# First layer's modulation vectors: more of their rows on VectorE, fewer and larger visits on TensorE

## The chip, the cores and the metric

The kernel runs on one core of a Trainium2 chip. The metric is device time in microseconds (us) of one execution, the median of several. TensorE (PE in the profile) does the matmuls; VectorE (DVE) and ScalarE (ACT) work on tiles in SBUF and on the matmuls' results in PSUM; SyncE (SP, its queue is SPq) issues the transfers from HBM, in the order in which they stand in its program. GpSimd does nothing here.

## The reference

Two layers of a diffusion backbone, float32 in and out, 256 latent tokens and 256 context tokens of 2048 channels. Each layer modulates its normalised input by vectors that it first computes from a conditioning vector (one for the latent stream, one for the context):

```
shift, scale, gate = split(silu(c) @ ada_w[l] + ada_b[l], 3)
h  = rmsnorm(x,  norm_g[l]) * (1 + scale)   + shift
hc = rmsnorm(xc, norm_g[l]) * (1 + scale_c) + shift_c
... = split(h @ w_in[l])        # then attention, pooling, Fourier mixing, gate, w_out
```

`ada_w[l]` is 2048 x 6144. For layer 0, nothing of the input projection can start before shift and scale are there, so the kernel computes these 4096 columns (33.5 MB of weights) piece by piece while it already multiplies the channels whose modulation is known. Two vectors (latent and context) are multiplied by each weight, so this product is bound by reading the weights, not by arithmetic.

## The kernel before, in words

**Pieces.** Activations lie with channels on the 128 partitions: 16 tiles of 128 channels by 512 tokens (`KT = 16`). In `startup` (lines 743 to 926) the 16 tiles are taken in ten groups, `GROUPS = (1, 1, 2, 2, 2, 2, 2, 2, 1, 1)`, numbered 0 to 9 below. A group of two tiles needs 512 columns of `ada_w` (256 shift, 256 scale), over 2048 contraction rows. The rows are cut in quarters; a quarter is one transfer of 1 MB (512 KB in a group of one tile) into the tile `a0`. This document writes **piece 5.1** for quarter 1 of group 5. The tile `a0` has four buffers (`ST = 4`), shared by all pieces: a transfer into a buffer waits until the last reader of that buffer's earlier contents is done.

**On TensorE**, a piece is one visit (line 891): four float32 matmuls, side by side in four 32-column strips of the array, with the conditioning vectors `cs` as the stationary operand. Between visits `work(n)` puts out `n` matmuls of the backlog (line 828): the first layer's input projection, three float32r products per term, over the channel tiles that are ready. After the last visit of a group ScalarE copies the sums from PSUM (`ev`, line 894), and four matmuls with a 0/1 matrix `selt` (line 897) turn the row vectors to columns and add the four strips. VectorE adds the bias and the norm's gain (lines 902 to 910), giving `ab`.

**Modulation.** `make_h` (line 244) multiplies a tile by the inverse root mean square (line 249), scales and shifts it per channel (VectorE in layer 0, line 256; ScalarE in layer 1, line 254), and `split` makes of it the float32r pair `h.hi` (ScalarE cast, line 139) and `h.lo` (VectorE subtraction, line 140). The weights go through the same `split`; their transfers (`raw`, line 146), casts `whi` and subtractions `wlo` have three buffers each.

**On VectorE.** In groups 5 to 9 (`JD = 5`) one quarter of each group isn't visited by TensorE: `dvec` (line 847) fetches it in another layout, and VectorE multiplies it by the conditioning row `cq` and sums it (line 859, 4 instructions for each tile of the group, eight in a group of two). `dvec(j + 1)` is called before the last visit of group `j`.

**Order.** In `startup` TensorE's order is the order in which the code calls it (a manual schedule). The other engines, and SyncE's transfers among them, are ordered by a scheduler when the program is built; the VectorE sums have a low priority there (`DLOW`). Once built, every engine's order is fixed, and each runs its own list from the top and stops at the first instruction that has to wait. After `startup` come layer 0's mixers, its output projection, and layer 1, where TensorE is busy throughout and VectorE computes the remaining modulation columns (line 189).

Of the kernel before, what the change touches and what calls it, by code (L numbers as in the profile page):

```python
# [32 lines left out]
KS = 8  # L33
DK = 3
JD = 5
KG = 4
# [20 lines left out]
def backbone(  # L57
# [18 lines left out]
    cc: bass.AP,  # L76
    sel: bass.AP,
    ident: bass.AP,
# [31 lines left out]
    nc.sync.dma_start(vt, vec)  # L110
    abq = const.tile([P, 2, KT, 2], F32, name="abq")
    xk = [ap_.tile([P, 4, T], F32, tag=f"A{g}", name=f"x0_{g}") for g in range(4)]
# [133 lines left out]
    def make_h(h, k, x, rstd, l, vs=(0, 1)):  # L246
        xn = x if vs == (1,) else t2("xn", (P, T))
        al = slice(vs[0] * N, vs[-1] * N + N)
        V.tensor_mul(xn[:, al], x[:, al], rstd[:, al])
        for v in vs:  # L250
            c = slice(v * N, v * N + N)
            a1, a0 = ab[l][:, 1, k, v : v + 1], ab[l][:, 0, k, v : v + 1]
            if l == 1:
                S.activation(xn[:, c], xn[:, c], AF.Identity, bias=a0, scale=a1)
            else:
                V.tensor_scalar(xn[:, c], xn[:, c], a1, a0, op0=ALU.mult, op1=ALU.add)
        split(xn[:, al], h.hi[k][:, al], h.lo[k][:, al])
# [478 lines left out]
    for g in range(3):  # L736
        load_x(g, 2)
    cq = f4("cq", (P, 2, 512), F32)
    nc.sync.dma_start(selt, sel)
    h0 = H(T, "h")  # L740


    def startup():
        st = tc.tile_pool(name="st", bufs=ST)
        with st as st:
# [102 lines left out]
            def dvec(j):  # L848
                if j == JD:
                    for v in range(2):  # L850
                        nc.sync.dma_start(cq[:, v], late["cd"][v, 1536:].partition_broadcast(P))
                gs, k0, pi = GROUPS[j], sum(GROUPS[:j]), start[j]
                n = P * gs * 1024
                raw = st.tile([P, 2 * gs, 512], F32, tag="a0", name=name("a0"))
                nc.sync.dma_start(raw, ada0[pi : pi + n].rearrange("(p b r) -> p b r", b=2 * gs, r=512))
                with tc.high_priority(offset=DLOW):
                    for q in range(2 * gs):
                        for v in range(2):
                            V.scalar_tensor_tensor(
                                t2("junk") if v == 0 else raw[:, q], raw[:, q], 1.0, cq[:, v], op0=ALU.mult, op1=ALU.mult,  # L860
                                accum_out=abq[:, q // gs, k0 + q % gs, v : v + 1],
                            )

            with tc.manual_schedule(engines={mybir.EngineType.PE}):
                for g in range(3):
                    stats(g)
                for j, gs in enumerate(GROUPS):
                    a = smt()
                    w_ = 256 * gs
                    npc = 4  # L870
                    kp = 4
                    k_first = 1 if j >= JD else 0
                    for kk in range(k_first, npc):
                        if j == 0 and kk == 1:
                            load_x(3, 1)
                        if kk == DK and JD <= j + 1 < len(GROUPS):
                            dvec(j + 1)
                        raw = st.tile([P, kp, w_], F32, tag="a0", name=name("a0"))
                        pi = start[j] + kk * P * kp * w_
                        nc.sync.dma_start(raw, ada0[pi : pi + P * kp * w_].rearrange("(p k n) -> p k n", k=kp, n=w_))  # L880
                        now[0] = 4 * j + kk
                        if kk == (PFK if j else 3):
# [5 lines left out]
                        for i in range(kp):  # L888
                            k = (kk * kp - kp + i) % KT
                            g = k % 4  # L890
                            PE.matmul(a[32 * g : 32 * g + 32, :w_], cs[:, k], raw[:, i], start=kk == k_first, stop=kk == npc - 1, tile_position=(0, 32 * g))  # L891
                        work(RATE * gs // 2)
                    ev = t2("ev")
                    S.copy(ev[:, :w_], a[:, :w_])
                    work(4)
                    for q in range(2 * gs):
                        PE.matmul(a[:, 2 * q : 2 * q + 2], ev[:, q * P : q * P + P], selt, start=True, stop=True)
                    work(4)
                    for w in range(2):
                        dst = ab[0][:, w, k0 : k0 + gs]  # L900
                        b0 = w * KT + k0
                        V.tensor_add(
                            dst, a[:, 2 * gs * w : 2 * gs * w + 2 * gs].rearrange("p (k v) -> p k v", v=2),
                            adab[:, b0 : b0 + gs].unsqueeze(2).to_broadcast([P, gs, 2]),
                        )
# [63 lines left out]
def _tables():  # L969
# [26 lines left out]
    rope = np.stack([c4, s4]).astype(f4).reshape(2, 2, P, P).transpose(2, 0, 1, 3)  # L996
    sel = np.zeros((P, 2), f4)
    sel[0::32, 0] = 1
    sel[1::32, 1] = 1
    return dict(rope=rope, band=band, icnt=icnt, dft0=dft0, cc=cc, sel=sel, ident=np.eye(P, dtype=f4))  # L1000


def _layout(x, c, ctx, c_ctx, ada_w, ada_b, norm_g, w_in, q_norm_g, k_norm_g, pool_w, pool_scale, fourier_w, w_out, final_norm_g):
# [14 lines left out]
    ps, k0 = [], 0  # L1018
    for gs in GROUPS:
        c = slice(k0 * P, (k0 + gs) * P)  # L1020
        a0 = np.concatenate([ada_w[0, :, :D][:, c], ada_w[0, :, D : 2 * D][:, c]], 1)
        last = a0[1536:]
        ps.append((last.reshape(512, 2 * gs, P).transpose(2, 1, 0) if len(ps) // 2 >= JD else last.reshape(4, P, 256 * gs).transpose(1, 0, 2)).reshape(-1))
        ps.append(a0[:1536].reshape(3, 4, P, 256 * gs).transpose(0, 2, 1, 3).reshape(-1))
        k0 += gs
# [41 lines left out]
```

## Time and profile before

| what | us |
|---|---|
| median of 3 runs (1084.06 to 1085.44) | 1084.48 |
| the profiled execution | 1083.26 |
| its span, first to last instruction | 1081.4 |
| `startup`'s backlog ends (last line 828 matmul) | about 173 |
| TensorE busy, 60 to 160 us | 100.0 of 100 |
| VectorE busy, 60 to 160 us | 64.7 of 100 |
| DMA share, 20 to 60 us / 60 to 120 us / 120 to 140 us | 1.02 / 0.88 to 0.93 / 0.51 |

The page's times are from the start of the span. A line such as `PE sm L891 x8` is eight records of the instructions of line 891 that write tile `sm`; a float32 matmul leaves two records, a float32r matmul or a transpose one. `[7.30 <-ACT whi L139]` says that the engine had been idle for 7.30 us and that the instruction of line 139 which writes `whi` ended the idling. PEclk is the clock that TensorE was granted, 1.00 at full speed.

### The profile page before, as it was taken

Reading aid. Unit: us, or ns where it says so; the run is one execution under the profiler, and the core shown is the slowest. Engines: PE = TensorE matmul, PEld = TensorE weight load, DVE = VectorE, ACT = ScalarE, POOL = GpSimd, SP = SyncE. Lnnn points to the kernel's source line nnn. Section 1 sums busy time; section 2 is a strip of 40 time slices with the busy share of each in tenths; the row PEclk is TensorE's granted clock in tenths of the full one; section 3 lists DMA queues with packets and bytes.
Section 4 is the critical chain, followed back from the end, with each engine's and each line's share of the span. In section 5 each row is a group of like instructions: output and inputs, shape, how many; then the busy total and the mean of one; then the engine's idle time right before and its main releaser. Section 6 shows DMA issues by size and latency. Waiting matters only on the chain.

```text
span 1081.4 us, 14324 instructions
## 1 busy us (share of the span) xinstructions
PE 1052.2 (97%) x5212; PEld 850.8 (79%) x5212; DVE 851.9 (79%) x1587; ACT 483.6 (45%) x809; POOL 0.2 (0%) x4
## 2 busy tenths in 40 slices
PE   5999999999999999999999999999999999999995
PEld 3566677888787888888888888888888888888884
DVE  6447556998999879998999887499657898878665
ACT  5223235323314675642532223288335758457551
POOL 0000000000000000000000000000000000000000
PEclk9899999999999999999999999999999999999998
DMA  9998677456685244457776557445755455765553
GB/s 358 408 342 340 230 253 252 156 197 228 211 262 169 98 137 145 158 189 268 267 285 206 195 195 260 139 149 176 264 196 185 168 199 168 260 206 181 190 184 90
DMA packets 66598, 231.56 MB, mean 214 GB/s; under 512 B 7200, under 2 KB 12384, under 8 KB 62944
## 3 DMA queue, kind: packets, MB, share of 16 engines
q1 hardware_dynamic: 66528, 230.65, 61.4%
q8 instruction: 41, 0.67, 0.3%
q14 instruction: 29, 0.24, 0.1%
HBM read 228.50 MB, written 2.11 MB: 213 GB/s over the span
## 4 chain that ended last, share of the span: by engine, by line
PE 86%; DVE 7%; issue 3%; DMA 2%; ACT 1%; SPq 0%; DVEq 0%; ACTq 0%
PE mm L338 16%; PE mm L336 16%; PE mm L337 16%; PE mm L312 10%; PE mm L828 7%; PE mm L313 5%; PE sm L828 4%; DVE ajunk L189 3%; PE sm L891 3%; PE sm L337 2%; PE sm L338 2%; PE sm L336 2%; PE sm L557 1%; DVE wlo L140 1%; DMA x<-in_xT 1%
## 5 line engine op out<-in xcount | busy, mean ns | idle before, releaser
L139 ACT CAST whi<-raw 128x1024 fp32r<-128x1024 f32 (+1 forms) x216 | 220.0, 1019 | 334.1 <-PE mm L337 111.5
L140 DVE TENSOR_TENSOR wlo<-raw,whi 128x1024 fp32r<-128x1024 f32 (+1 forms) x216 | 255.4, 1183 | 93.9 <-ACT whi L139 92.5
L189 DVE SCALAR_TENSOR_TENSOR ajunk<-araw,cbt 128x1024 bf16<-128x1024 f32 x224 | 273.9, 1223 | 47.7 <-DMA araw<-in_adar 33.7
L336 PE MATMUL mm<-whi,h 128*128 128x512 f32 x416 | 167.4, 403 | 0.0
L338 PE MATMUL mm<-whi,h 128*128 128x512 f32 x416 | 162.9, 392 | 0.0
L337 PE MATMUL mm<-wlo,h 128*128 128x512 f32 x416 | 162.9, 392 | 0.0
L336 PE MATMUL mm<-m,whi 128*128 128x512 f32 (+1 forms) x272 | 102.6, 377 | 0.0
L337 PE MATMUL mm<-m,whi 128*128 128x512 f32 (+1 forms) x272 | 102.4, 377 | 0.0
L338 PE MATMUL mm<-m,wlo 128*128 128x512 f32 (+1 forms) x272 | 102.4, 376 | 0.0
L312 PE MATMUL mm<-h,whi 128*128 128x512 f32 x256 | 92.6, 401 | 0.0
L338 PEld LDWEIGHTS mm<-whi,h 128*128 128x128 f32 x416 | 78.1, 188 | 17.0 <-DVE h L140 0.3
L336 PEld LDWEIGHTS mm<-whi,h 128*128 128x128 f32 x416 | 78.2, 188 | 15.9 <-issue 1.4
L312 PE MATMUL mm<-m,whi 128*128 128x512 f32 x256 | 90.7, 400 | 0.0
L337 PEld LDWEIGHTS mm<-wlo,h 128*128 128x128 f32 x416 | 78.2, 188 | 15.7 <-issue 1.4
L336 PE MATMUL mm<-h,whi 128*128 128x512 f32 x196 | 77.6, 396 | 0.0
L338 PE MATMUL mm<-h,wlo 128*128 128x512 f32 x196 | 76.8, 392 | 0.0
L337 PE MATMUL mm<-h,whi 128*128 128x512 f32 x196 | 76.7, 392 | 0.0
L313 PE MATMUL mm<-h,wlo 128*128 128x256 f32 x256 | 72.4, 283 | 0.0
L313 PE MATMUL mm<-m,wlo 128*128 128x256 f32 x256 | 71.7, 281 | 0.0
L828 PE MATMUL mm<-whi,h 128*128 128x512 f32 x192 | 65.3, 409 | 1.3 <-ACT h L139 1.3
L336 PEld LDWEIGHTS mm<-m,whi 128*128 128x128 f32 x272 | 51.2, 188 | 9.5
L337 PEld LDWEIGHTS mm<-m,whi 128*128 128x128 f32 x272 | 51.2, 188 | 9.4
(206 smaller groups left out, 1624.7 us busy)
## 6 DMA issues: line engine op xcount, KB each, us to landing
araw<-in_adar SPq DMA_DIRECT2D x128, 512.0 KB, 4.2
raw<-in_wb SPq DMA_DIRECT2D x78, 512.0 KB, 4.2
raw<-in_wo SPq DMA_DIRECT2D x64, 512.0 KB, 4.3
raw<-in_wg SPq DMA_DIRECT2D x55, 512.0 KB, 4.4
a<-in_ada SPq DMA_DIRECT2D x24, 1024.0 KB, 7.3
a<-in_ada SPq DMA_DIRECT2D x16, 512.0 KB, 4.6
x<-in_xT SPq DMA_DIRECT2D x4, 1024.0 KB, 6.0
cbt<-cd SPq DMA_DIRECT2D x7, 512.0 KB, 5.4
```

The source lines that it names most:

```text
L139: i = S.copy(hi, src)
L140: V.tensor_sub(lo, src, hi.bitcast(F32))
L189: V.scalar_tensor_tensor(junk, raw, 1.0, cbt[:, v], op0=ALU.mult, op1=ALU.mult, accum_out=acc[:, u, h, v : v + 1])
L312: PE.matmul(a.rearrange("p (s n) -> p s n", s=2), hi[:, j - j0], h.both[k][:, :, :N], start=s0, stop=False)
L313: PE.matmul(a[:, :N], lo[:, j - j0], h.hi[k][:, :N], start=False, stop=s1)
L336: PE.matmul(o, ah, bh, start=start, stop=False)
L337: PE.matmul(o, ah, bl, start=False, stop=False)
L338: PE.matmul(o, al, bh, start=False, stop=stop)
L557: PE.transpose(tp[:, h * P : h * P + P], ps[h][:, i * P : i * P + P], idt)
L828: PE.matmul(o, lt, r, start=s0, stop=s1)
L891: PE.matmul(a[32 * g : 32 * g + 32, :w_], cs[:, k], raw[:, i], start=kk == k_first, stop=kk == npc - 1, tile_position=(0, 32 * g))
```

## The change

`ND = (0, 0, 0, 0, 1, 2, 1, 2, 2, 2)` says how many of each group's four quarters VectorE takes, in place of `JD`: one in groups 4 and 6, two in groups 5, 7, 8 and 9. Of the 40 pieces, TensorE visits 30 where it visited 35; of the five it gives up, those of groups 4, 5 and 7 are 1 MB, those of groups 8 and 9 512 KB. Where two or fewer pieces are left to TensorE, they are visited one right after the other, without backlog matmuls between, and the 42 (in a group of one tile: 21) backlog matmuls follow. The sums need a second conditioning row tile `cq`. The products with `selt` become transposes (`idt`), and VectorE adds the strips by one reduction; the `+1` of the scale is added once, ahead. `make_h` modulates every tile but the first on ScalarE.

```diff
-            if l == 1:
+            if l == 1 or k:
                 S.activation(xn[:, c], xn[:, c], AF.Identity, bias=a0, scale=a1)
...
             def dvec(j):
+                gs, k0, n = GROUPS[j], sum(GROUPS[:j]), P * GROUPS[j] * 1024
+                for e in range(ND[j]):
+                    if ND[j - 1] < ND[j] and not used[e]:
+                        used[e] = True
                         for v in range(2):
+                            nc.sync.dma_start(cq[e][:, v], late["cd"][v, 1536 - 512 * e : 2048 - 512 * e].partition_broadcast(P))
+                    raw = st.tile([P, 2 * gs, 512], F32, tag="a0", name=name("a0"))
+                    pi = start[j] + (3 - e) * n
+                    nc.sync.dma_start(raw, ada0[pi : pi + n].rearrange("(p b r) -> p b r", b=2 * gs, r=512))
+                    with tc.high_priority(offset=DLOW):
+                        for q in range(2 * gs):
+                            for v in range(2):
+                                V.scalar_tensor_tensor(
+                                    t2("junk") if v == 0 else raw[:, q], raw[:, q], 1.0, cq[e][:, v], op0=ALU.mult, op1=ALU.mult,
+                                    accum_out=abq[:, e, q // gs, k0 + q % gs, v : v + 1],
+                                )
...
+                    npc = 4 - ND[j]
+                    raws = []
+                    for kk in range(npc):
...
+                        if kk == npc - 1 and j + 1 < len(GROUPS):
                             dvec(j + 1)
+                        raws.append(piece(j, kk))
...
+                        if npc > 2:
+                            ada_part(a, raws[kk], kk, kk == 0, kk == npc - 1, w_)
+                            work(RATE * gs // 2)
+                    if npc <= 2:
+                        for kk in range(npc):
+                            ada_part(a, raws[kk], kk, kk == 0, kk == npc - 1, w_)
+                        work(3 * RATE * gs // 2)
...
                     for q in range(2 * gs):
-                        PE.matmul(a[:, 2 * q : 2 * q + 2], ev[:, q * P : q * P + P], selt, start=True, stop=True)
+                        PE.transpose(a[:, q * P : q * P + P], ev[:, q * P : q * P + P], idt)
                     work(4)
...
+                    V.tensor_reduce(
+                        red.rearrange("p w k v -> p (w k) v"), a[:, :w_].rearrange("p (q g r) -> p q r g", g=4, r=32)[:, :, 0:2, :],
+                        axis=AX.X, op=ALU.add,
+                    )
...
+                    for e in range(ND[j]):
+                        V.tensor_add(red, red, abq[:, e, :, k0 : k0 + gs])
+                    V.tensor_add(dst, red, bias.unsqueeze(3).to_broadcast([P, 2, gs, 2]))
+                    V.tensor_mul(dst[:, 1], dst[:, 1], ng[:, k0 : k0 + gs].unsqueeze(2).to_broadcast([P, gs, 2]))
```

After `startup` every engine's list is the same as before. Inside it, two places matter below. In the rows, `DMAHW`n is a count of landed transfers, `PE_49` and `DVE_49` counts of finished instructions of the engine named; a row without `PE` or `DVE` waits for no reader.

**Group 7, SyncE's list.** Before, the pieces that TensorE reads are `a0_168` (7.1), `a0_172` (7.2) and `a0_179` (7.3), and VectorE's for group 8 is `a0_176`:

```order
L880 DMA a0_168_944<-in_ada0 128x2048 [waits DMAHW0_49,PE_49]
L146 DMA raw_169_953<-in_wb 128x1024 [waits DMAHW7_49,DVE_49]
L880 DMA a0_172_970<-in_ada0 128x2048 [waits DMAHW2_49,PE_49]
L146 DMA raw_173_989<-in_wgs 128x768 [waits DMAHW1_49,DVE_49]
L855 DMA a0_176_996<-in_ada0 128x1024 [waits DMAHW4_49,PE_49]
L880 DMA a0_179_1004<-in_ada0 128x2048 [waits DMAHW3_49,DVE_49]
```

Now TensorE reads `a0_189` (7.0) and `a0_196` (7.1), and VectorE's for group 8 are `a0_190` and `a0_193`:

```order
L869 DMA a0_189_962<-in_ada0 128x2048 [waits DMAHW2_49,DMAHW0_49,PE_49]
L854 DMA a0_190_964<-in_ada0 128x1024 [waits DMAHW6_49,PE_49]
L143 DMA raw_197_1007<-in_wb 128x1024 [waits DVE_49]
L143 DMA raw_200_1037<-in_wgs 128x768 [waits DMAHW3_49,DVE_49]
L143 DMA raw_216_1114<-in_wb 128x1024 [waits DMAHW7_49,DMAHW4_49,DVE_49]
L854 DMA a0_193_972<-in_ada0 128x1024 [waits DMAHW5_49,DMAHW0_49,PE_49]
L869 DMA a0_196_980<-in_ada0 128x2048 [waits DVE_49]
```

and TensorE's list there reads

```order
L910 MATMUL sm_164_829<-idt_89,ev_181_924 128x128 x4
L825 MATMUL mm_153_759<-wlo_160_799,h_7_120 128x512
L825 MATMUL mm_153_759<-whi_159_798,h_7_120 128x512
L825 MATMUL mm_150_756<-whi_159_798,h_8_121 128x512
L825 MATMUL mm_150_756<-wlo_160_799,h_8_121 128x512
L874 MATMUL sm_188_961<-a0_189_962,cs_137 32x512 x4
L874 MATMUL sm_188_961<-a0_196_980,cs_137 32x512 x4
```

The two visits of group 7 have come to stand back to back, and the buffer of `a0_193` is the one that `a0_189` had: the count that its transfer waits for is reached by the last of the four matmuls that read `a0_189`. `a0_196`, the second piece of the same pair of visits, stands behind it in SyncE's list.

**Groups 4 and 5, SyncE and VectorE.** Before, VectorE sums one piece per group and its list holds eight sums between other work; SyncE's list, in which `a0_137` is VectorE's piece of group 6 and `a0_142` TensorE's 5.3, reads

```order
L880 DMA a0_136_728<-in_ada0 128x2048 [waits DMAHW4_49,PE_49]
L855 DMA a0_137_748<-in_ada0 128x2048 [waits DMAHW5_49,DMAHW0_49,PE_49]
L880 DMA a0_142_762<-in_ada0 128x2048 [waits DMAHW7_49,DMAHW6_49,DVE_49]
L146 DMA raw_143_775<-in_wb 128x1024 [waits Activation_49]
L880 DMA a0_150_825<-in_ada0 128x2048 [waits DMAHW2_49,PE_49]
```

Now `a0_121` and `a0_126` are VectorE's two pieces of group 5, `a0_131` is TensorE's last piece of group 4 (4.2), `a0_140` and `a0_146` are 5.0 and 5.1, and `a0_141` is VectorE's piece of group 6:

```order
L854 DMA a0_121_615<-in_ada0 128x2048 [waits DMAHW7_49,DMAHW5_49,DVE_49]
L851 DMA cq_4_117<-cd_108 128x512 [waits DMAHW6_49]
L851 DMA cq_4_117<-cd_108 128x512
L854 DMA a0_126_631<-in_ada0 128x2048 [waits DMAHW0_49,PE_49]
L869 DMA a0_131_645<-in_ada0 128x2048 [waits DMAHW2_49,DMAHW1_49,PE_49]
L143 DMA raw_132_652<-in_wb 128x1024 [waits Activation_49]
L869 DMA a0_140_703<-in_ada0 128x2048 [waits DMAHW4_49,DMAHW3_49,PE_49]
L854 DMA a0_141_705<-in_ada0 128x2048 [waits DMAHW5_49,DVE_49]
L869 DMA a0_146_719<-in_ada0 128x2048 [waits DMAHW1_49,PE_49]
```

Here `a0_121` waits for VectorE's last sum over group 4's piece, and `a0_141` for its last sum over `a0_121`. Between these two sums VectorE's list has, in this order, two products of line 246, a `wlo` of 1024 columns, group 3's reduction and two small operations, two `h.lo`, and then

```order
L858 SCALAR_TENSOR_TENSOR junk_122_617,abq_84<-a0_121_615,cq_3_116 128x512
L137 TENSOR_TENSOR wlo_119_589<-raw_117_586,whi_118_588 128x768
L858 SCALAR_TENSOR_TENSOR a0_121_615,abq_84<-a0_121_615,cq_3_116 128x512
L858 SCALAR_TENSOR_TENSOR junk_123_620,abq_84<-a0_121_615,cq_3_116 128x512
L858 SCALAR_TENSOR_TENSOR junk_124_623,abq_84<-a0_121_615,cq_3_116 128x512
L858 SCALAR_TENSOR_TENSOR a0_121_615,abq_84<-a0_121_615,cq_3_116 128x512 x2
L858 SCALAR_TENSOR_TENSOR junk_125_626,abq_84<-a0_121_615,cq_3_116 128x512
L858 SCALAR_TENSOR_TENSOR junk_127_633,abq_84<-a0_126_631,cq_4_117 128x512
L858 SCALAR_TENSOR_TENSOR junk_128_636,abq_84<-a0_126_631,cq_4_117 128x512
L858 SCALAR_TENSOR_TENSOR a0_126_631,abq_84<-a0_126_631,cq_4_117 128x512 x2
L858 SCALAR_TENSOR_TENSOR a0_121_615,abq_84<-a0_121_615,cq_3_116 128x512
```

Four sums over the second piece have come to stand ahead of the last one over the first. In the list before, all eight sums of a piece follow each other.

More of the change, by code (lines that the diff above doesn't have):

```diff
@@ L33 @@
 KS = 8
-DK = 3
-JD = 5
+ND = (0, 0, 0, 0, 1, 2, 1, 2, 2, 2)
 KG = 4
@@ L76, in backbone @@
     cc: bass.AP,
-    sel: bass.AP,
     ident: bass.AP,
@@ L737, in backbone @@
         load_x(g, 2)
-    cq = f4("cq", (P, 2, 512), F32)
-    nc.sync.dma_start(selt, sel)
+    cq = [f4("cq", (P, 2, 512), F32) for _ in range(2)]
     h0 = H(T, "h")
@@ L848, in dvec @@
             def dvec(j):
[L849 to L857, printed above, removed]
-                        for v in range(2):
[L859 to L862, printed above, removed]
+                gs, k0, n = GROUPS[j], sum(GROUPS[:j]), P * GROUPS[j] * 1024
@@ new lines, in startup, with piece, ada_part @@
+            used = [False, False]
+            def piece(j, kk):
+                n, w_ = P * GROUPS[j] * 1024, 256 * GROUPS[j]
+                raw = st.tile([P, 4, w_], F32, tag="a0", name=name("a0"))
+                pi = start[j] + kk * n
+                nc.sync.dma_start(raw, ada0[pi : pi + n].rearrange("(p k n) -> p k n", k=4, n=w_))
+                return raw
+            def ada_part(a, raw, kk, first_, last, w_):
+                for i in range(4):
+                    PE.matmul(
+                        a[32 * i : 32 * i + 32, :w_], cs[:, 4 * kk + i], raw[:, i], start=first_, stop=last, tile_position=(0, 32 * i)
+                    )
@@ L869, in startup @@
                     w_ = 256 * gs
[L870 to L873, printed above, removed]
+                    npc = 4 - ND[j]
+                    raws = []
+                    for kk in range(npc):
                         if j == 0 and kk == 1:
                             load_x(3, 1)
-                        if kk == DK and JD <= j + 1 < len(GROUPS):
+                        if kk == npc - 1 and j + 1 < len(GROUPS):
                             dvec(j + 1)
[L878 to L882, printed above, removed]
+                        raws.append(piece(j, kk))
+                        now[0] = 4 * j + kk + 4 - npc
+                        if kk + 4 - npc == (PFK if j else 3):
                             queue(4 * j + 4 + (QK if j else Q0), k0, gs)
@@ L887, in startup @@
                             nc.sync.dma_start(idt, ident)
[L888 to L892, printed above, removed]
+                        if npc > 2:
[5 more added lines that the diff above has]
+                        work(3 * RATE * gs // 2)
                     ev = t2("ev")
@@ L1018, in _layout @@
     ps, k0 = [], 0
[L1019 removed]
+    for gs, nd in zip(GROUPS, ND):
         c = slice(k0 * P, (k0 + gs) * P)
         a0 = np.concatenate([ada_w[0, :, :D][:, c], ada_w[0, :, D : 2 * D][:, c]], 1)
[L1022 to L1024 removed]
+        for q in range(4):
+            w = a0[512 * q : 512 * q + 512]
+            ps.append((w.reshape(512, 2 * gs, P).transpose(2, 1, 0) if q >= 4 - nd else w.reshape(4, P, 256 * gs).transpose(1, 0, 2)).reshape(-1))
         k0 += gs
```

27 lines of the change are left out of this document (8 added, 19 removed).

## The prediction

> **What bounds the kernel now.** I read the page first: TensorE is busy 97% of the span, so only a stretch where TensorE waits, or work taken off it, can change the time. Then the windows, to see what limits `startup`:
>
> ```profile
> span 1081.4 us, 14324 instructions
> PE 1052.2 (97%) x5212; PEld 850.8 (79%) x5212; DVE 851.9 (79%) x1587; ACT 483.6 (45%) x809; POOL 0.2 (0%) x4
> ...
> 40.00:60.00 20.00, 18.86 (x99) 10.01 (x98) 7.99 (x17) 4.80 (x7) 0.00 (x0) 0.91 1.02 419
> 60.00:80.00 20.00, 20.00 (x105) 12.92 (x104) 10.71 (x25) 5.98 (x10) 0.00 (x0) 1.00 0.93 328
> 80.00:100.00 20.00, 20.00 (x103) 13.87 (x101) 15.39 (x39) 7.38 (x11) 0.00 (x0) 1.00 0.88 323
> 100.00:120.00 20.00, 20.00 (x107) 13.04 (x108) 14.96 (x43) 6.11 (x8) 0.00 (x0) 1.00 0.88 337
> ```
>
> Up to 60 us the transfers are saturated. From there TensorE is busy without a gap, at full clock, while VectorE (third busy figure) has a quarter to a half of its time free. Here a visit that goes is time won, provided that the pieces still arrive in time. The chain of waits gives the prices (start, us, what; the last row is from the attention stage):
>
> ```profile
> 47.02 3.28 PE sm L891 x16
> 63.67 0.79 PE sm L897 x8
> 65.51 0.99 PE sm L891 x8
> 66.50 3.42 PE sm L828 x14
> 84.02 0.79 PE sm L897 x8
> 141.78 0.34 PE sm L897 x4
> 143.17 0.57 PE sm L891 x8
> 157.17 5.44 PE mm L828 x24
> 369.10 0.44 PE sm L557 x4
> ```
>
> **What TensorE saves.** Visits: three pieces of 1 MB at 0.99 and two of 512 KB at 0.57, 4.1 us. Broken runs: 24 backlog matmuls in a row take 5.44, 0.227 each, so 14 would take 3.17, but 14 between two visits take 3.42; each break costs 0.25. Group 4 loses one break, groups 5, 7, 8 and 9 two each: 9 x 0.25 = 2.2 us. Transposes: four products with `selt` took 0.79, four float32 transposes take 0.44 at line 557. That is 0.35 in each of groups 3 to 7 and, by halves, 0.12 in groups 8 and 9: 2.0 us, all on the bounding engine. In groups 0 to 2 it would be another 0.6, where part of it may go under in transfer waits (bounds 0 and 0.9). Sum: 4.1 + 2.2 + 2.0 + 0.6 = **8.9 us saved** if nothing waits.
>
> **What the other engines get.** VectorE has 32 sums more and 30 modulations less, ScalarE the modulations:
>
> ```profile
> 58.41 0.96 DVE L140 TENSOR_TENSOR wlo<-raw,whi 128x768 fp32r<-128x768 f32 x1 [7.30 <-ACT whi L139]
> 59.28 1.29 DVE L249 TENSOR_TENSOR xn<-x,rstd 128x512 f32<-128x512 f32 x2
> ...
> 79.45 0.69 DVE L859 SCALAR_TENSOR_TENSOR junk<-a,cq 128x512 f32<-128x512 f32 x1
> 80.06 0.69 DVE L859 SCALAR_TENSOR_TENSOR a<-a,cq 128x512 f32<-128x512 f32 x1
> ...
> 84.85 0.23 DVE L902 TENSOR_TENSOR ab<-sm,vt 128x4 f32<-128x4 f32 x2 [0.73 <-PE sm L897]
> 113.25 1.23 DVE L140 TENSOR_TENSOR wlo<-raw,whi 128x1024 fp32r<-128x1024 f32 x1 [1.75 <-ACT whi L139]
> ...
> L256 DVE TENSOR_SCALAR xn<-xn,ab 128x256 f32<-128x256 f32 x31 | 10.9, 410 | 0.3
> L139 ACT CAST h<-xn 128x512 fp32r<-128x512 f32 x15 | 9.3, 620 | 19.0 <-DVE xn L256 18.8
> L254 ACT ACTIVATE xn<-xn,ab 128x256 f32<-128x256 f32 x16 | 8.8, 594 | 0.1
> ```
>
> A sum starts 0.61 after the one before: 32 x 0.61 = 19.5 us more for VectorE, 10.5 less for the modulations (10.9 x 30/31). On average there is room. ScalarE gets 30 x 0.59 = 18 us where it is a third busy. I cost both at nothing in themselves; what they cost is lateness, and only where TensorE waits for it. A pair of tiles' `h` comes about 1.3 us later than now, since ScalarE needs 0.59 for what VectorE did in 0.35 (10.9 / 31). But TensorE first uses group 3's `h` after two more visits and 28 backlog matmuls, some 9 us after the transposes; that lateness is covered (uncovered, at most 1.3 us per group).
>
> **Where a stall goes in: group 7.** This term rests on order, not on load. TensorE reads piece 7.0 and at once 7.1. SyncE may issue VectorE's `a0_193` only when the last matmul on 7.0 is done, and 7.1 (`a0_196`) stands behind it. So between the two visits lies a whole transfer, whatever is early or late elsewhere. Behind the waiting matmul stands all of TensorE's backlog, and behind that the copy `ev` and group 7's `h`. Its price, from SyncE's timeline and the landing times of four transfers (the landing rows belong, in order, to the issues at 79.77, 81.41, 111.68 and 112.10):
>
> ```profile
> 79.77 0.33 SPq L855 DMA_DIRECT2D a<-in_ada  x1
> 81.41 0.33 SPq L880 DMA_DIRECT2D a<-in_ada  x1
> ...
> 111.68 0.33 SPq L855 DMA_DIRECT2D a<-in_ada  x1
> 112.10 0.38 SPq L880 DMA_DIRECT2D a<-in_ada  x1
> ...
> a<-in_ada SPq DMA_DIRECT2D x1, 1024.0 KB, 4.9
> a<-in_ada SPq DMA_DIRECT2D x1, 1024.0 KB, 6.9
> a<-in_ada SPq DMA_DIRECT2D x1, 512.0 KB, 4.6
> a<-in_ada SPq DMA_DIRECT2D x1, 1024.0 KB, 7.3
> ```
>
> At 111.68 the same pair goes out, 512 KB and 0.42 later 1 MB; the second lands 7.3 after its issue, 7.7 after the start, but behind other traffic. Alone, 1 MB landed in 4.9: 0.4 + 4.9 = 5.3 is the floor. I take **7.0** (5.3 to 8), nearer the pair, since a weight transfer waiting for VectorE stands just ahead of it too.
>
> **Groups 4 and 5.** Piece 5.1 stands in SyncE's list behind `a0_141`, which waits for VectorE's last sum over `a0_121`. When is that? The `wlo` at 58.41 stays where it is (it hangs on TensorE), and ends at 59.28. Then eight sums of group 4 (4.9) to 64.2; two line 249 products (1.2) to 65.4; a `wlo` of 1024 (1.15) to 66.5; reduction and two small operations (0.2 each) to 67.1. ScalarE: three activations and a cast (2.4), then another of each (1.2), to 70.7; the second `h.lo` on VectorE (0.6) to 71.4. Then twelve sums and a `wlo` of 768: 12 x 0.61 + 0.87 = 8.2, to 79.6. `a0_141` is issued at 79.7, 5.1 at 80.1. `a0_141` lands at 84.6 (4.9), 5.1 one megabyte later: at 419 GB/s 2.5, so 87.1. When does TensorE want it? It leaves the transposes at 64.1 and does 54 backlog matmuls in five runs (12.2 + 1.3), four visits (4.0) and four transposes (0.4): 82.0. **Stall 5.1 us.** Bounds: 5.1 alone on the queue, 85.0, stall 3.0; or as the pair at 79.77 and 81.41 did, whose second landed at 88.3, 8.5 after the first issue: 88.2, stall 6.2. Part of it already falls before piece 4.2, whose transfer is issued behind `a0_121`, `cq` and `a0_126`, from 64.2 on: three and a half megabytes, to about 76, where TensorE is there at 74. The sum of both stalls stays 5.1, since 5.1's landing hangs on VectorE.
>
> **What a stall does to the clock.** One-microsecond windows around two early pauses:
>
> ```profile
> 26.00:27.00 1.00, 0.84 (x2) 0.75 (x3) 0.78 (x3) 0.95 (x3) 0.00 (x0) 0.50 1.10 442
> 30.00:31.00 1.00, 1.00 (x10) 0.48 (x3) 0.00 (x0) 0.00 (x0) 0.00 (x0) 0.81 0.99 401
> ...
> 45.00:46.00 1.00, 0.48 (x5) 0.48 (x5) 0.00 (x0) 0.47 (x1) 0.00 (x0) 1.00 1.10 447
> 46.00:47.00 1.00, 0.58 (x6) 0.51 (x6) 0.28 (x3) 0.00 (x0) 0.00 (x0) 1.00 1.01 422
> 48.00:49.00 1.00, 1.00 (x8) 0.27 (x4) 0.96 (x4) 0.85 (x2) 0.00 (x0) 0.50 1.03 414
> 50.00:51.00 1.00, 1.00 (x6) 0.69 (x3) 0.96 (x2) 0.12 (x1) 0.00 (x0) 0.57 0.99 410
> ```
>
> After two microseconds that were half idle the granted clock is 0.50 for about three: the two visits at 47.02 take 3.28 where two at 0.99 would take 1.98. One drop costs 1.5. After the longer pause at 25 us work resumes at 26.2 and the full clock at 30.4, so 2.1. I take 1.5 for groups 4 and 5 (bounds 0 and 1.7) and 1.8 for group 7 (1.5 to 2.1). [...]
>
> **Sum.** -8.9 + 5.1 + 1.5 + 7.0 + 1.8 = **+6.5 us**. The profiled execution took 1083.26 (1.9 outside its span), so 1089.8; the median of the runs is 1.2 above it, so **1091.0**. After `startup` every engine's list is unchanged and TensorE bounds, so I let the difference through whole. The ends of the terms give 3.0 + 0 + 5.3 + 1.5 - 9.2 = 0.6 slower and 6.2 + 1.7 + 8 + 2.1 - 8.3 = 9.7 slower: 1085.1 to 1094.2.
>
> **Rivals.**
> - *Short stalls keep the clock* (two stalls under 3 us, no drop): +5.0, 1089.5. For it: neither stall alone is as long as the pause at 25 us. Against: the drop at 47.
> - *The lateness runs on into groups 8 and 9*: 16 sums per group of two (9.8 us) fill VectorE, pieces 8.1 and 9.1 stand behind `a0_212` and group 9's sums, and one more stall like that of group 5 arises: +5.1, 1096.1. Against: after 7.1 TensorE has 46 backlog matmuls (10.4 us) before it wants 8.1, while VectorE catches up in the stall.
> - *VectorE keeps up*: 5.1 lands before 82.0, if the sums over group 4 start before 58.4 or the engine's small operations cost less. Then only group 7 stalls: -8.9 + 7.0 + 1.8 = -0.1, 1084.4, no change. Against: VectorE's list has that `wlo` ahead of the sums.
> - *Faster: the stalls find cover*, the saving comes through: -8.9, 1075.6. It decides from the point where 7.1 is in its buffer before 7.0 is read; I see no way to that in the list, only an error of mine in who waits for whom. With group 5's stall in place the change is clearly faster only if group 7's is gone altogether (-8.9 + 5.1 + 1.5 = -2.3).
>
> **How the numbers follow.** Forecast 0.45, clock rival 0.22, lateness rival 0.13, VectorE keeps up 0.12, faster 0.08. About 0.2% (2.2 us) can be told from no change: slower from 1086.7. The first three are slower, but for the forecast's low end: 0.78; within, the fourth and that end: 0.13; faster: 0.09. The range runs from the fourth case to the third: 1084.0 to 1096.0, the forecast's own inside it.
>
> **What would show it.** Right: a gap of 5 to 8 us on TensorE between its two visits of group 7, ended by the landing of `a0`; waits for `a0` before 4.2 and 5.1 of 5 us together; granted clock 0.50 after them; line 910 at about 0.11 each; `startup`'s end near 180 in place of 173. Wrong: 7.1 landed when 7.0 is read; VectorE done with `a0_121` well before 79; a TensorE that waits for `h`; full clock after the stalls.

## The result and the profile after

The change made the kernel slower: 1093.72 us (median of 11 runs, 1087.66 to 1096.62) against 1084.88 (11 runs, 1084.06 to 1086.55), a ratio of 1.0067, 95% interval 1.0049 to 1.0086. The forecast was 1091.0. A later set of six runs of the changed kernel, on one chip, gave 1089.77, ratio 1.0058 (1.0040 to 1.0075). The profiled execution of the change took 1089.94 us, its span 1088.2, which is 6.8 more than the span before. One of the twelve runs of the kernel with five buffers (below) took 1172.28 us at a mean clock of 0.845, where the others have 0.987 to 0.991, and its ratio leaves that run out.

First the windows after, with the same columns as before (PE, PEld, DVE, ACT and POOL busy, granted clock, DMA share, GB/s):

```profile
span 1088.2 us, 14228 instructions
PE 1042.1 (96%) x5140; PEld 846.6 (78%) x5140; DVE 860.8 (79%) x1612; ACT 497.1 (46%) x839; POOL 0.2 (0%) x4
...
40.00:60.00 20.00, 16.50 (x92) 8.21 (x91) 8.97 (x18) 6.45 (x11) 0.00 (x0) 1.00 1.01 402
60.00:80.00 20.00, 16.36 (x79) 9.98 (x78) 16.64 (x48) 7.74 (x13) 0.00 (x0) 0.94 0.94 345
80.00:100.00 20.00, 18.57 (x88) 13.65 (x89) 13.41 (x33) 8.10 (x15) 0.00 (x0) 0.97 0.96 378
100.00:120.00 20.00, 18.18 (x96) 11.22 (x94) 17.58 (x51) 7.85 (x13) 0.00 (x0) 1.00 0.77 265
120.00:140.00 20.00, 13.47 (x51) 9.65 (x52) 13.86 (x36) 4.94 (x8) 0.00 (x0) 0.74 0.75 279
140.00:160.00 20.00, 20.00 (x115) 15.13 (x114) 9.19 (x24) 9.29 (x17) 0.00 (x0) 1.00 0.50 163
```

TensorE is busy 10.1 us less than before in the whole span, and yet later: between 60 and 140 us, where it had been busy throughout, it now stands still for 13.4 us. TensorE's timeline says where; the rows are the visits (line 874) and one of the rows of transposes (line 910), with the idle time before them in brackets:

```profile
46.11 1.92 PE L874 MATMUL sm<-a,cs 128*32 128x512 f32 x16 [0.35 <-DVE red L913]
...
58.63 1.07 PE L874 MATMUL sm<-a,cs 128*32 128x512 f32 x8 [1.79 <-DMA a<-in_ada]
...
63.84 0.60 PE L910 MATMUL sm<-idt,ev 128*128 128x128 f32 x4
...
77.89 1.93 PE L874 MATMUL sm<-a,cs 128*32 128x512 f32 x8 [3.61 <-DMA a<-in_ada]
...
86.05 1.06 PE L874 MATMUL sm<-a,cs 128*32 128x512 f32 x8
...
88.55 1.06 PE L874 MATMUL sm<-a,cs 128*32 128x512 f32 x8 [1.43 <-DMA a<-in_ada]
...
117.22 1.07 PE L874 MATMUL sm<-a,cs 128*32 128x512 f32 x8
126.53 1.94 PE L874 MATMUL sm<-a,cs 128*32 128x512 f32 x8 [8.24 <-DMA a<-in_ada]
```

In order: group 3's first two visits; 3.3; group 3's transposes; 4.2; 5.0 and 5.1; 7.0 and 7.1. Four visits wait for their piece, 1.79 + 3.61 + 1.43 + 8.24 = 15.1 us. Nothing waits for `h` there. SyncE's timeline shows why 4.2, 5.1 and 7.1 are late: 4.2 is the row at 66.53, behind VectorE's two pieces of group 5, and landed 11.3 us later; 5.1 is the row at 79.88, right behind `a0_141` at 78.64; and 7.1 is the first of the two transfers at 118.73, right behind `a0_193` at 118.35, which could go out only when 7.0 had been read.

```profile
66.53 0.33 SPq L869 DMA_DIRECT2D a<-in_ada  x1
...
78.64 0.33 SPq L854 DMA_DIRECT2D a<-in_ada  x1
79.88 0.33 SPq L869 DMA_DIRECT2D a<-in_ada  x1
...
118.35 0.33 SPq L854 DMA_DIRECT2D a<-in_ada  x1
118.73 0.90 SPq L869 DMA_DIRECT2D a<-in_ada  x2
```

After 4.2 and after 7.1 TensorE resumes at half clock (granted clock 0.50). One-microsecond windows:

```profile
77.00:78.00 1.00, 0.11 (x4) 0.11 (x8) 1.00 (x5) 0.00 (x0) 0.00 (x0) 0.87 1.02 430
78.00:79.00 1.00, 1.00 (x8) 0.09 (x8) 1.00 (x3) 0.00 (x0) 0.00 (x0) 0.50 0.63 266
...
81.00:82.00 1.00, 1.00 (x5) 0.79 (x5) 1.00 (x3) 0.00 (x0) 0.00 (x0) 0.92 0.90 377
...
126.00:127.00 1.00, 0.47 (x4) 0.20 (x8) 1.00 (x2) 0.00 (x0) 0.00 (x0) 0.50 0.74 225
...
130.00:131.00 1.00, 1.00 (x4) 0.80 (x3) 1.00 (x5) 0.00 (x0) 0.00 (x0) 0.50 0.87 311
...
132.00:133.00 1.00, 1.00 (x5) 0.83 (x4) 0.10 (x2) 0.18 (x1) 0.00 (x0) 0.82 0.45 168
```

A visit takes 1.93 us there, against 1.07 at full clock. Half clock while it works, from 77.9 to 81.2 and from 126.5 to 132.4, costs 3.3 / 2 = 1.6 and 5.9 / 2 = 2.9 us. Where `startup` ends, the first matmul of the next stage shows; the first fence is the kernel before, the second the change:

```profile
175.82 0.39 PE L828 MATMUL sm<-h,wlo 128*128 128x512 f32 x1
176.05 0.39 PE L336 MATMUL mm<-whi,h 128*128 128x512 f32 x1
```

```profile
184.81 0.39 PE L825 MATMUL sm<-h,wlo 128*128 128x512 f32 x1
185.03 0.39 PE L333 MATMUL mm<-whi,h 128*128 128x512 f32 x1
```

So `startup` ends 9.0 us later (at 175.8 before, not at the "about 173" that was read off the chain of waits). Counted from the traces over all of `startup`, from TensorE's first matmul on: TensorE stands still for 5.2 us before and for 21.7 after, and 8.7 us of its work run at half clock before and 12.5 after. (Before, half clock lasts from 23.5 to 30.4 and from 47.4 to 50.9; after, from 26.6 to 30.0 and in the two stretches above. The drop at 47.4 is gone: the two visits at 46.11 take 1.92 where those at 47.02 took 3.28.) Waiting costs 16.5 more, of which 15.1 are the four waits above, and the clock 3.8 / 2 = 1.9 more, 18.4 in all. Since the end moves by only 9.0, TensorE's work, put at full clock, is 9.4 shorter, where 8.9 was forecast; the other two traces of the change give 9.0 and 10.1.

### The profile page after: what moved, and what is told of

It reads as the page before. It is cut to its first block, busy times and chain, and to the rows that moved or that the text cites. A ratio compares the mean times of both kernels' runs of the same rounds, so it can differ in the third digit from the quotient of the medians.

```text
span 1088.2 us, 14228 instructions
## 1 busy us (share of the span) xinstructions
PE 1042.1 (96%) x5140; PEld 846.6 (78%) x5140; DVE 860.8 (79%) x1612; ACT 497.1 (46%) x839; POOL 0.2 (0%) x4
## 4 chain that ended last, share of the span: by engine, by line
PE 64%; DVE 7%; issue 3%; DMA 1%; ACT 1%; DVEq 0%; SPq 0%; ACTq 0%
PE mm L333 14%; PE mm L335 14%; PE mm L334 14%; PE mm L309 10%; PE mm L310 5%; DVE ajunk L186 2%; PE sm L334 2%; PE sm L335 2%; PE sm L333 2%; DVE wlo L137 2%; PE sm L554 1%; DMA araw<-in_adar 1%; DMA cbt<-cd 1%; PE sm L517 1%; DVE ss L465 0%
## 5 line engine op out<-in xcount | busy, mean ns | idle before, releaser
L136 ACT CAST whi<-raw 128x1024 fp32r<-128x1024 f32 (+1 forms) x216 | 219.9, 1020 | 333.4 <-PE mm L334 105.2
L334 PEld LDWEIGHTS mm<-m,whi 128*128 128x128 f32 x272 | 51.2, 188 | 9.5
L335 PEld LDWEIGHTS mm<-m,wlo 128*128 128x128 f32 x272 | 51.2, 188 | 9.4
```

The source lines that it names most:

```text
L136: i = S.copy(hi, src)
L334: PE.matmul(o, ah, bl, start=False, stop=False)
L335: PE.matmul(o, al, bh, start=False, stop=stop)
```

## The experiments

The theory was that the pieces' order of issue and their buffers make the loss, and that the saving is real. The rivals: lateness that VectorE hands on, ScalarE's modulation, the number of buffers. Each edit is shown against the changed kernel unless said otherwise; each ratio is to runs of the kernel before in the same set.

| kernel | median us | ratio to before (95%) |
|---|---|---|
| the change | 1093.72 | 1.0067 (1.0049 to 1.0086) |
| the change, later set | 1089.77 | 1.0058 (1.0040 to 1.0075) |
| 7.1 ahead of VectorE's pieces | 1081.84 | 0.9983 (0.9969 to 0.9997) |
| last piece ahead in every group | 1080.69 | 0.9964 (0.9951 to 0.9976) |
| VectorE's old shares | 1077.29 | 0.9933 (0.9921 to 0.9945) |
| five buffers | 1083.87 | 0.9995 (0.9983 to 1.0007) |
| old shares, VectorE modulates | 1077.83 | 0.9936 (0.9924 to 0.9948) |
| last piece ahead, one quarter each | 1081.33 | 0.9976 (0.9965 to 0.9987) |
| last piece ahead, two in groups 8, 9 | 1082.56 | 0.9983 (0.9972 to 0.9995) |
| before + transposes alone | 1079.35 | 0.9958 (0.9946 to 0.9971) |
| one quarter each, own order | 1079.76 | 0.9958 (0.9946 to 0.9971) |
| old shares, two in group 9 | 1076.69 | 0.9932 (0.9918 to 0.9945) |

**Group 7's order alone.**

```diff
+                        if j == 7 and kk == npc - 1:
+                            raws.append(piece(j, kk))
                         if kk == npc - 1 and j + 1 < len(GROUPS):
                             dvec(j + 1)
-                        raws.append(piece(j, kk))
+                        if j != 7 or kk != npc - 1:
+                            raws.append(piece(j, kk))
```

> The change with one call moved: in group 7 alone piece 7.1 is asked for ahead of VectorE's two pieces of group 8, so its issue waits only for the last matmul on piece 6.2 (about 111.5 us) instead of the last matmul on 7.0 and VectorE's sums. Theory (the queue and buffer order makes group 7's gap): the 8.24 us gap shrinks to at most 1 us and the clock drop of 2.9 us behind it goes: 8.2 + 2.9 = 11 less, 1093.7 - 11 = 1082.7 us, range 1081.5 to 1085. Rival 1 (the lateness is only handed on, to groups 8 and 9, because VectorE's pieces of group 8 now come later): at least 5 us of the 11 come back as waits in groups 8 and 9, 1088 us or more. Rival 2 (the gap has little to do with the order, TensorE would have waited for h anyway): 1092 to 1094.

Measured: 1081.84 us. The gap is gone; TensorE's two visits of group 7 stand in one row, no clock drop follows (the single matmuls behind them stay at 0.39 us), and of waits for pieces behind them there is one of 1.10 us, in group 8:

```profile
115.81 1.92 PE L874 MATMUL sm<-a,cs 128*32 128x512 f32 x16
...
131.89 0.64 PE L874 MATMUL sm<-a,cs 128*32 128x256 f32 x8 [1.10 <-DMA a<-in_ada]
```

Both rivals fall. Group 7's order is worth 0.84% (1.0067 to 0.9983), 9 us, and by itself turns the change from slower to just faster (the interval ends at 0.9997). For this very case, group 7's stall gone and group 5's in place, the prediction had -2.3 us; the medians give -2.7.

**The same move in every group.**

```diff
+                        raws.append(piece(j, kk))
                         if kk == npc - 1 and j + 1 < len(GROUPS):
                             dvec(j + 1)
-                        raws.append(piece(j, kk))
```

> The same move in every group: the last piece of each group that TensorE visits is asked for ahead of VectorE's pieces of the next group. Theory: the waits of pieces 3.3 (1.8 us), 4.2 (3.6), 5.1 (1.4) and 7.1 (8.2) all shrink to nearly nothing, with the clock drops behind 4.2 (1.65) and 7.1 (2.9): 19.6 us less than the change, 1074 us, range 1072 to 1079; a clock drop may return in group 3 as before (1.7). Rival 1 (VectorE, whose pieces now arrive later, becomes the bound: sums late, first add of abq late, then h and the backlog): 1080 to 1088 with waits of TensorE on h or on the reduction in groups 4 to 9. Rival 2 (the stalls did not carry the loss): within 2 us of 1093.7.

Measured: 1080.69 us, 6.7 more than the theory said, within the first rival. The theory was right on the pieces and wrong on what follows. The waits by what ended them:

```profile
PE sm L874 <- DVE red L913: 8.0, 6, 2.6
PE sm L874 <- DMA a<-in_ada: 1.1, 2, 0.6
```

Waits for pieces all but vanish, and 8.0 us of waits for the reduction take their place. VectorE's pieces now come last, and VectorE comes to the reduction later. Group 3's transposes start at 63.81 on TensorE; VectorE, in its fixed order, has a `wlo`, two sums and two products ahead of the reduction, at 66.88, and TensorE's first visit of group 4 (piece 4.0), which writes an `sm` buffer, waits for it. VectorE's timeline first, then TensorE's:

```profile
63.31 1.23 DVE L137 TENSOR_TENSOR wlo<-raw,whi 128x1024 fp32r<-128x1024 f32 x1
64.45 0.68 DVE L858 SCALAR_TENSOR_TENSOR a<-a,cq 128x512 f32<-128x512 f32 x1
...
65.06 0.68 DVE L858 SCALAR_TENSOR_TENSOR junk<-a,cq 128x512 f32<-128x512 f32 x1
...
65.67 1.28 DVE L246 TENSOR_TENSOR xn<-x,rstd 128x512 f32<-128x512 f32 x2
66.88 0.18 DVE L913 TENSOR_REDUCE red<-sm 128x8 f32<-128x32 f32 x1
```

```profile
63.81 0.66 PE L910 MATMUL sm<-idt,ev 128*128 128x128 f32 x4 [1.20 <-ACT ev L907]
...
67.11 1.07 PE L874 MATMUL sm<-a,cs 128*32 128x512 f32 x8 [1.71 <-DVE red L913]
```

**The edits without the larger shares.**

```diff
-ND = (0, 0, 0, 0, 1, 2, 1, 2, 2, 2)
+ND = (0, 0, 0, 0, 0, 1, 1, 1, 1, 1)
```

> The change with VectorE's shares of before (one quarter of groups 5 to 9, none of group 4): what stays is the transposes in place of the select products, ScalarE modulating the tiles, the merged reduction and adds, and the placing of VectorE's quarter. Theory: these edits are worth the 2.0 + 0.6 us counted for the transposes and groups 0 to 2: 1084.9 - 2.6 = 1082.3 us, range 1080.5 to 1084.5. Rival (one of these edits makes h later, ScalarE's modulation above all, and is itself part of the loss): 1085 to 1090, with TensorE waits on h.

Measured: 1077.29 us, 0.67% faster than before, 7.3 us where 2.6 was expected. TensorE is busy 99.97 of the 100 us from 60 to 160 and its waits for pieces sum to 1.2 us. So the other edits are no part of the loss, and the larger shares cost 1.34% (0.9933 to 1.0067), 14.5 us. Of the 5.8 us that its span is shorter than before, 3.4 are won in `startup` (2.4 less work on TensorE, 1.7 less lost at half clock, 0.7 more waiting) and 2.4 after it, in lists that didn't change.

**Five buffers.** `cs` moves to the pool of the large tiles, which has room.

```diff
-ST = 4
+ST = 5
...
-            cs = st.tile([P, KT, 32], F32, tag="cs", bufs=1, name="cs")
+            cs = f4("cs", (P, KT, 32), F32)
```

> The change with five buffers of the a0 tile instead of four (the small tile cs moves to another pool to make room), the order of the issues left as it is. Theory (the order binds, the number of buffers only in part): piece 7.1 still waits for the last matmul on 7.0, so group 7 keeps a gap of 6 to 8 us; VectorE's first piece of group 5 is issued some 3 us earlier, so the waits before 4.2 and 5.1 lose 3 to 5 us of their 5: 1087 to 1091 us. Rival (the number of buffers is the cause as such): the group 7 gap goes too, 1083 us or less.

Measured: 1083.87 us, below the range of the theory. The waits before 4.2 and 5.1 are 1.48 and 1.29, 2.3 less than in the first trace of the change, where 3 to 5 was expected. A gap in group 7 stays, so it isn't the buffer count as such; but it is 4.85 us, not 6 to 8:

```profile
121.39 1.93 PE L874 MATMUL sm<-a,cs 128*32 128x512 f32 x8 [4.85 <-DMA a<-in_ada]
```

With a fifth buffer VectorE's second piece goes out earlier, and only 7.1 still waits until 7.0 is read; 4.85 us is about what 1 MB took alone in the kernel before (4.9). By this the other 3.4 of the 8.24 would be due to VectorE's transfer ahead of it and the traffic beside it.

**The old shares with VectorE modulating** (against the kernel with the old shares):

```diff
-            if l == 1 or k:
+            if l == 1:
```

> The kernel with VectorE's old shares (1077.3 us) and VectorE, not ScalarE, modulating the tiles of the first layer. It asks where that kernel's 5 us beyond the forecast come from. Theory (they are not the modulation's: VectorE had idle time there): within 1 us of 1077.3. Rival (ScalarE's modulation frees VectorE and brings h earlier): 1080 to 1084, with TensorE waits on h.

Measured: 1077.83 us, ratio 0.9936 against 0.9933. Who modulates makes no difference that can be measured; the theory holds.

**The transposes alone**, in the kernel before:

```diff
-                        PE.matmul(a[:, 2 * q : 2 * q + 2], ev[:, q * P : q * P + P], selt, start=True, stop=True)
+                        PE.transpose(a[:, q * P : q * P + P], ev[:, q * P : q * P + P], idt)
...
+                    V.tensor_reduce(
+                        red.rearrange("p w k v -> p (w k) v"), a[:, :w_].rearrange("p (q g r) -> p q r g", g=4, r=32)[:, :, 0:2, :],
+                        axis=AX.X, op=ALU.add,
+                    )
...
-                            dst, a[:, 2 * gs * w : 2 * gs * w + 2 * gs].rearrange("p (k v) -> p k v", v=2),
+                            dst, red[:, w],
```

> The kernel before with one part of the change alone: transposes and a reduction over the four row groups in place of the select products; the shares, the visits, the adds behind the reduction and the modulation on VectorE stay. It asks how much of the 7.3 us that the kernel with the old shares gains is the transposes'. Theory (they were costed right, at 2.0 us, and the rest is the clock drop of group 3 and later time): 1082.3 us, range 1081 to 1083.5. Rival (all the gain comes with them, the clock drop of group 3 included): 1077 to 1079.

Measured: 1079.35 us, 4.5 faster, between the theory and the rival. Rows of the kernel before, then of this one: the next row starts 0.81 us after four `selt` products, but 0.35 after four transposes, so a group of two gains 0.46 where 0.35 was costed. Group 3's two visits have full clock (2.02 us):

```profile
63.51 0.95 PE L897 MATMUL sm<-selt,ev 128*128 128x2 f32 x8
64.32 0.49 PE L828 MATMUL sm<-h,whi 128*128 128x512 f32 x1
```

```profile
48.52 2.02 PE L891 MATMUL sm<-a,cs 128*32 128x512 f32 x16 [0.35 <-DVE red L900]
...
63.91 0.60 PE L897 MATMUL sm<-idt,ev 128*128 128x128 f32 x4
64.26 0.48 PE L828 MATMUL sm<-h,whi 128*128 128x512 f32 x1
```

Its span is 4.2 us shorter, and only 2.2 of that are won in `startup`: 3.4 less work on TensorE and 0.9 less lost at half clock (the drop in group 3 is gone), against 2.0 more waiting, above all 3.20 for `h` at 28.39, and a start 0.1 later. Of the 2.0 after `startup`, 1.9 come in the last stage, whose pace differs from run to run (last section). So 3.4 us of work are the transposes' own; what else of the 4.5 is theirs stays open. The remaining 0.25% to the kernel with the old shares (0.9958 to 0.9933) wasn't taken apart.

**One quarter each, in the change's own order.**

```diff
-ND = (0, 0, 0, 0, 1, 2, 1, 2, 2, 2)
+ND = (0, 0, 0, 0, 1, 1, 1, 1, 1, 1)
```

> The change in its own order of issue, but never more than one quarter of a group for VectorE: one each of groups 4 to 9. Against the kernel with the old shares only group 4's quarter is added. Theory (one quarter costs VectorE and the a0 queue nothing but piece 3.3's wait of 1.8 us behind the two cq rows and VectorE's piece, against one visit of 1.0 us saved): 1078.1 us, range 1077 to 1079.5. Rival 1 (the quarter of group 4 is itself a good part of the change's loss, as lateness that runs on): 1081 or more. Rival 2 (the wait finds cover): 1076.3.

Measured: 1079.76 us, just outside the theory's range; waits for pieces are 2.3 us in all, where the old shares have 1.2. Group 4's quarter brings nothing, and costs 0.25% against the old shares; but most of the loss comes from the second quarters.

**One quarter each with the last piece ahead**, and **two quarters in groups 8 and 9 alone with the last piece ahead**: the move of the second experiment, with other shares.

```diff
-ND = (0, 0, 0, 0, 1, 2, 1, 2, 2, 2)
+ND = (0, 0, 0, 0, 1, 1, 1, 1, 1, 1)
```

> TensorE's last piece asked for first in every group, and VectorE has one quarter of each of the groups 4 to 9, never two. Theory (with half of the sums VectorE no longer runs late, so the 8 us of waits on the reduction go, and the order of issue keeps the pieces in time): waits on pieces and on the reduction under 2 us in all, against the kernel with the old shares one visit of 1.0 us less: 1076.3 us, range 1075 to 1078. Rival (the waits on the reduction do not come from VectorE's sums): 1079 us or more, with waits of 1 to 2.6 us on the reduction in groups 4 to 8.

```diff
-ND = (0, 0, 0, 0, 1, 2, 1, 2, 2, 2)
+ND = (0, 0, 0, 0, 0, 1, 1, 1, 2, 2)
```

> As the last, but VectorE has none of group 4, one quarter of groups 5 to 7 and two of the small groups 8 and 9 only, so group 7 stays in three visits. Theory: two visits of 0.5 us and two breaks of 0.3 us fewer than with the old shares, 1075.7 us, range 1074.5 to 1078. Rival (two quarters are too much for VectorE there too, or the order of a0 stalls groups 8 and 9): 1078 us or more, with waits in groups 8 and 9.

Measured: 1081.33 and 1082.56 us; both theories fell, and the times and the longest waits (1.72 us in group 4; 2.42 in group 9) are as the rivals said. The move costs more than it saves: 3.1 and 3.8 us of waits on the reduction, and a clock drop in each: in the first the granted clock is 0.50 from 68.6 us on; in the second a matmul of `h` and `wlo` takes 0.63 us at 146.70, behind the wait of 2.42, and 0.39 at 147.74. With half of the sums the waits on the reduction are 3.1 us in place of 8.0, which fits VectorE's sums as a part of their cause, but not as all of it: with one quarter each, two sums and two products still stand ahead of group 3's reduction, which starts at 67.14. With one quarter each, the change's own order is, if anything, the better one (0.9958 against 0.9976); its waits on the reduction are 1.2 us.

**The old shares and a second quarter in the last group.**

```diff
-ND = (0, 0, 0, 0, 1, 2, 1, 2, 2, 2)
+ND = (0, 0, 0, 0, 0, 1, 1, 1, 1, 2)
```

> The old shares, and a second quarter for VectorE in the last group alone, where VectorE was busy less than half of the time before; the order of issue as in the change. Theory (one visit of 0.5 us and one break of 0.3 us less, and nothing behind it to stall): 1076.5 us, range 1075.5 to 1077.5. Rival (piece 9.1 now waits for VectorE's sum over the first quarter of group 9, or the last reduction waits for the sums): 1078 to 1081, with a wait in group 9.

Measured: 1076.69 us, ratio 0.9932. It beats both kernels, as does the one with the old shares, from which it can't be told apart (0.9933).

**The change twice more**, unaltered, for the spread of its runs.

> The changed kernel once more, as it is, for a second trace: its runs spread over 9 us (1087.7 to 1096.6), those of before over 2.5, and the longer ones have the lower mean clock (0.984 against 0.988). Theory (the stalls are as long each time, and what varies is for how long the clock stays at half after them): the waits before pieces 3.3, 4.2, 5.1 and 7.1 are within 0.7 us of the first trace's 1.8, 3.6, 1.4 and 8.2, and each us of the span beyond 1088.2 goes with 2 us more at half clock. Rival (the transfers vary): the waits themselves are longer by the difference in time.

> The changed kernel once more, timed, for a third trace. The second trace came out 1.6 us shorter than the first, with waits 2.0 us shorter in all, nearly all of it before piece 4.2 (1.7 in place of 3.6). Theory (the waits hang on how long transfers take beside each other, and with them the spread): the third trace's span differs from 1088.2 by the difference of its waits for a0 (16.3 in the first) and half the difference in time at half clock while TensorE works, within 1.5 us; the median lies at 1088 to 1095. Rival (the waits are the same each time and the spread is made after startup): the waits within 0.5 us of one of the first two traces, and the span off by 2 us or more from what they say.

Measured: 1088.37 us with a span of 1086.6, and 1089.77 (median of six; the profiled execution took 1091.12, its span 1089.3). The waits move about. Before 3.3, 4.2, 5.1 and 7.1 the second trace has 2.29, 1.73, 1.17 and 7.92; the third has these rows (3.3, 4.2, 5.0, 5.1, 7.1):

```profile
59.86 1.93 PE L874 MATMUL sm<-a,cs 128*32 128x512 f32 x8 [2.48 <-DMA a<-in_ada]
...
77.47 1.07 PE L874 MATMUL sm<-a,cs 128*32 128x512 f32 x8 [0.41 <-DMA a<-in_ada]
...
85.71 1.07 PE L874 MATMUL sm<-a,cs 128*32 128x512 f32 x8 [1.47 <-DVE red L913]
...
89.38 1.94 PE L874 MATMUL sm<-a,cs 128*32 128x512 f32 x8 [2.61 <-DMA a<-in_ada]
...
127.66 1.93 PE L874 MATMUL sm<-a,cs 128*32 128x512 f32 x8 [6.42 <-DMA a<-in_ada]
```

The first expectation's theory, that the waits are the same each time, fell: in the second trace they are 2.0 us shorter and the span 1.6 shorter, as its rival said. In the third the waits are spread otherwise and the clock falls at other places (0.50 at 60 us, behind 3.3). The theory of the second expectation held there, at its edge: the waits for pieces are 1.5 us shorter (14.8 against 16.3) and half clock costs 1.1 more (14.8 us of work against 12.5), which makes -0.4; the span is 1.1 longer, and 1.5 was allowed. The theory left out the waits on the reduction, 1.5 more than in the first trace (2.2 against 0.7). In the first set the three slowest runs (1094.4 to 1096.6) are the three with the lowest mean clock, 0.984; no trace of one so long was taken, so why that set's median lies 4 us above the later one's stays open.

## Why the prediction was right, and where its terms were off

The sign, the place and the mechanism held. Term by term:

- **"What TensorE saves", 8.9.** 9.4 by the count in the traces. The transposes with the small groups were put at 2.6 and took 3.4 us of work off TensorE by themselves, since 0.35 a group was read off the chain of waits where the rows give 0.46. The step that failed is the one on the clock: it priced the drops that the new stalls would bring and used the pause at 45 us for that price, but didn't ask whether the change would take this very drop away. It did: 3.4 us at half clock, 1.7 us.
- **"Groups 4 and 5", 5.1.** 3.61 + 1.43 = 5.0 in the first trace. VectorE's last sum over `a0_121` was to end at 79.6 and 5.1 to go out at 80.1; they came at 78.6 and 79.88. But 5.1 landed only when its visit began, at 88.5, 8.6 after its issue, later than the 87.1 of the forecast, and TensorE came later too. The agreement is partly luck: the other two traces have 2.9, and 3.0 with another 1.5 for the reduction.
- **The wait before 3.3 was not in the sum**: 1.79, 2.29 and 2.48 in the three traces. The step missed is the rule to count every transfer that an edit sends ahead: VectorE's new piece of group 4 and the two `cq` rows now stand in front of 3.3, as a quarter of group 5 stood in front of 4.3 before.
- **The clock after groups 4 and 5, 1.5.** 1.6 in the first trace, 1.7 in the second; the third has two drops, behind 3.3 and behind 5.0, of 1.7 and 2.3.
- **"Where a stall goes in: group 7", 7.0** (5.3 to 8). 8.24, 7.92 and 6.42, 7.5 on average; the floor, one transfer alone, was 4.85 with five buffers. The order read from the lists was right in each step, and moving one call removed it.
- **The clock after group 7, 1.8** (1.5 to 2.1). 2.9 in the first trace (5.9 us of work at half clock), 2.3 and 1.9 in the others. The range was too narrow because the longest pause of the trace before was taken as its end.
- **"I let the difference through whole."** 9.0 at the end of `startup`, 6.8 in the span. Of the 2.2 made up, 1.5 come after 975 us, by a pace of matmuls that differs from run to run (below), so the sum of 6.5 met the profiled 6.8 partly by two errors that cancel: 2.5 too little in `startup`, 2.2 won later. The median's 8.8 is near the 9.0.

Of the rivals, *VectorE keeps up* and *the stalls find cover* didn't happen; the second would have taken the move of one call. *The lateness runs on into groups 8 and 9* didn't either: in the first trace no visit behind 7.1 waits for its piece. *Short stalls keep the clock* was half right. In the first trace the stalls of 1.79 and 1.43 kept full clock (1.00) and those of 3.61 and 8.24 lost it (0.50). Other runs disagree. The rows are one-microsecond windows: first of the kernel with one quarter each and the last piece ahead, with a wait of 1.72 us that ends at 67.38; then of the kernel with group 7's order moved, with a wait of 2.62 that ends at 87.15:

```profile
67.00:68.00 1.00, 0.62 (x8) 0.16 (x8) 1.00 (x5) 0.00 (x0) 0.00 (x0) 1.00 0.06 25
68.00:69.00 1.00, 1.00 (x9) 0.52 (x3) 0.18 (x2) 0.75 (x2) 0.00 (x0) 0.81 0.31 33
69.00:70.00 1.00, 1.00 (x3) 0.78 (x3) 0.00 (x0) 1.00 (x3) 0.00 (x0) 0.50 0.59 147
```

```profile
86.00:87.00 1.00, 0.00 (x0) 0.00 (x0) 1.00 (x6) 0.84 (x2) 0.00 (x0) 1.00 0.99 406
87.00:88.00 1.00, 0.85 (x8) 0.16 (x8) 1.00 (x5) 1.00 (x3) 0.00 (x0) 1.00 1.05 428
88.00:89.00 1.00, 1.00 (x8) 0.72 (x5) 1.00 (x3) 0.97 (x3) 0.00 (x0) 1.00 1.11 459
89.00:90.00 1.00, 1.00 (x6) 0.82 (x5) 1.00 (x4) 1.00 (x3) 0.00 (x0) 1.00 0.98 414
```

The shorter wait lost the clock and the longer kept it. The length of a single gap does not settle it here.

## What to carry to other kernels

Where transfers are issued in order from a ring of buffers, look up for each transfer which reader's end its buffer waits for, and what stands behind it: merging two visits put a whole transfer between them, and moving one call took 9 us of it back. Moving transfers ahead of each other is a trade, since the consumer that now gets its data later may be the one whose result releases the next buffer. Time taken off a bounding engine by a cheaper instruction (the transposes) showed in the kernel's time; time taken off by shifting work to an engine with idle time on average did not, because the order of the transfers and the ends of their buffers' readers, TensorE's own visit in group 7 and VectorE's sums in groups 4 and 5, decided when pieces came.

## What the runs showed of the hardware that was not expected

- **The longer wait did not always cost the clock.** The granted clock stayed at 1.00 behind a wait of 2.62 us (group 7's order moved) and fell to 0.50 behind one of 1.72 (one quarter each, last piece ahead). What a stall costs in clock was read off each trace here; it was not shown what decides it.
- **A drop came with short waits, and went with a small edit.** In the kernel before the clock fell at 47.4 us, behind waits of 0.71 and 0.44 us, and the two visits there took 3.28 us. With the transposes alone the waits are 0.71 and 0.35, and the visits take 2.02; in the change they are the same, and the visits take 1.92.
- **The last stage's matmuls went at two paces at the same granted clock, 1.00.** The change's delay shrinks from 8.3 us at 975 us to 6.8 at 1065, evenly, 1.5 us or 2% of the stage. The windows from 1000 to 1020 us show it in the number of records, of the change and then of the kernel with group 7's order moved (the kernel before shows 115 as well):

```profile
1000.00:1020.00 20.00, 20.00 (x117) 17.62 (x116) 13.70 (x19) 11.47 (x16) 0.00 (x0) 1.00 0.59 200
```

```profile
1000.00:1020.00 20.00, 20.00 (x115) 17.34 (x114) 12.54 (x17) 10.14 (x13) 0.00 (x0) 1.00 0.56 185
```

  In these windows one quarter each in its own order shows 117 too; the last piece ahead in every group and the old shares show 115. The stage's instructions are the same. The cause wasn't found.
